# Two blocks for the two parts of a split operand: where the FFNs' inputs and gated products lie in SBUF

## The chip, the cores and the metric

The kernel runs on one core of one Trainium2 chip. The metric is the device time of one execution in microseconds; the median of three runs of the kernel before is 960.75 us (959.98 to 960.87). A change of less than about 0.2% cannot be told from no change.

## What is computed

A trunk of two decoder layers on 256 positions of width 1024, all in float32. Each layer is half an FFN, a mixer and half an FFN again, with a root-mean-square norm ahead of each, and a last norm at the end. The mixer of the first layer is two causal convolutions side by side, that of the second an attention with 16 heads.

```python
def swiglu_ffn(x, w_gate_up, w_down):
    gate, up = jnp.split(x @ w_gate_up, 2, axis=-1)
    return (jax.nn.silu(gate) * up) @ w_down          # 1024 -> 2 x 2816 -> 1024

for layer in range(DEPTH):                            # DEPTH = 2
    x = x + 0.5 * swiglu_ffn(rms_norm(x, ffn1_norm[layer]), ...)
    x = x + mixer(rms_norm(x, mix_norm[layer]), ...)  # layer 0: convolutions, layer 1: attention
    x = x + 0.5 * swiglu_ffn(rms_norm(x, ffn2_norm[layer]), ...)
return rms_norm(x, final_norm)
```

## The kernel before

**Layout.** Everything is kept transposed: 128 channels on the partitions, the 256 positions along the free dimension. A weight tile of 128 x 128 is the stationary operand of a matmul, and 256 positions of activations are the moving one.

**The split.** A float32 operand is split into two float32r parts whose sum is the number: the first part is the number rounded (ScalarE), the second what is left (VectorE). `split` does so for the weights (`w1`, `w2`), `split_to` for activations. Two helpers then multiply split operands. `mm3` (L162, L163, L164) makes three matmuls of 256 columns: w1 by the first part, w1 by the second part, w2 by the first part. `mm2` (L168, L169) makes two: w1 by both parts at once, 512 columns, into the two halves of a PSUM bank, and w2 by the first part, 256 columns. The halves are added later (`join`, or two additions to x).

**Stages.** An FFN is two stages. In the input stage 22 panels multiply `norm.xs`, the split normed input (`xs`, 8 chunks of 128 channels), with gate and up: 16 pairs of mm2 a panel, or 16 triples of mm3 in the panels that `one` picks (L373). The result is scaled, gated and split into `gs`, the gated products (22 chunks). In the product stage each of eight output chunks sums 22 pairs over `gs`, the last one 22 triples. The four FFNs have numbers 0 to 3 in the order in which they run. The attention's queries and keys are also made by mm2 from `xs`, the convolution's inputs mostly by mm3.

**Places.** This is what the change touches. `xs` lies in `xs_all` (L173), a tile that begins at a multiple of 1024 bytes in each partition and is a little longer than needed, so that a stage may begin some bytes later. In `Norm.__init__` (L281) the layout is chunk by chunk: the first part of chunk 0 (256 elements, 1024 bytes), its second part, the first part of chunk 1, and so on. `XS_START` gives the place where this begins, for each FFN's first half (F1), the mixer (MX) and the second (F2), for the two layers. Since a part is 1024 bytes long, each first part and each second part of a stage begins at the same place modulo 1024. `GS_START` does the same for `gs` (L368), whose tile begins at 256 or 320 modulo 1024, so that all parts begin at 1056, that is 32. The weights' tiles begin at multiples of 1024, and so each 128 x 128 weight tile at 0 or 512.

In short, before: parts begin at 288 (inputs of FFNs 0 and 1), 32 (inputs of FFNs 2 and 3, and all products), 192 (the convolution's input), 256 (the attention's input), modulo 1024.

**Order.** `advance` loads units of 1 MB of weights ahead and splits them; SyncE's queue issues the loads. TensorE runs the matmuls in the order in which the code issues them.

Of the kernel before, what the change touches and what calls it, by code (L numbers as in the profile page):

```python
# [11 lines left out]
F32R = mybir.dt.float32r  # L12
# [5 lines left out]
P = 128  # L18
D = 1024
S = 256  # L20
DEPTH = 2
FF = 2816
ND = D // P
NF = FF // P
# [27 lines left out]
ONES = [4, 0, 0, 2]  # L52
ONE_END = 1
PRIO_F = 0
FFN_STEP = 40
# [4 lines left out]
WIDEC = 0  # L60
LINE = 1024
BASE = 16512
XS_START = {"F1": (288, 32), "MX": (192, 256), "F2": (288, 32)}
GS_START = (800, 800, 800, 736)
GROUPS = ((0, 2), (2, 4), (4, 6), (6, 8))
M_POOL = [0, 0, 0, 0]
B_POOL = [0, 0]
# [10 lines left out]
C_F1, C_MX, C_F2, C_FN = 0, DEPTH * ND, 2 * DEPTH * ND, 3 * DEPTH * ND  # L78
# [15 lines left out]
def trunk(ctx: ExitStack, tc: tile.TileContext, xin, wst, cst, bia, idn, out):  # L94
    nc = tc.nc
    keep = ctx.enter_context(tc.tile_pool(name="keep", bufs=1))
# [12 lines left out]
    at = {"load": 0, "split": 0}  # L109
# [20 lines left out]
    def advance(u, ahead_split=ahead_split):  # L130
        while at["load"] < min(n_units, u + ahead_load):
            load(at["load"])
            at["load"] += 1
        while at["split"] < min(n_units, u + ahead_split):
            split(at["split"])
            at["split"] += 1
# [3 lines left out]
    whole = {0} | {first_conv + i for i in WHOLE}  # L140

    class Stream:
        def __init__(self, u):
            self.u = u
# [8 lines left out]
    def take(n):  # L153
        st = Stream(used[0])
        used[0] += n
        return st

    def mm3(o, a, b, start, stop, check=False):
        if len(a) == 1:
            nc.tensor.matmul(o, a[0], b[-1], start=start, stop=stop, skip_group_check=check)  # L160
            return
        nc.tensor.matmul(o, a[0], b[0], start=start, stop=False, skip_group_check=check)  # L162
        nc.tensor.matmul(o, a[0], b[1], start=False, stop=False, skip_group_check=check)  # L163
        nc.tensor.matmul(o, a[1], b[0], start=False, stop=stop, skip_group_check=check)  # L164
# [5 lines left out]


    x = keep.tile([P, ND, S], F32, name="x")
    xs_all = keep.tile([P, ND * 2 * S + LINE // 4], F32R, name="xs")  # L173
    const_all = keep.tile([P, LINE // 4], F32, name="const")
    const = const_all[:, :NCONST]
    ident = keep.tile([P, P], F32, name="ident")
# [101 lines left out]
    class Norm:  # L278


        def __init__(self, col, whole=None, start=0):  # L281
            self.col, self.whole = col, whole
            self.xs = xs_all[:, start // 4:start // 4 + ND * 2 * S].rearrange(
                "p (d t s) -> p d t s", d=ND, t=2)
            self.sums = tmp.tile([P, S], F32, name="sums")

        def add(self, d):
# [23 lines left out]
    def twice(r):  # L311
        return r[:, None, :].to_broadcast([P, 2, S])

    def project(st, base, xs, xg=None):

        bank = psa.tile([P, 2, S], F32, name="pa")
        for i in range(2):
            for k in range(ND):
                w = st.tile(base + 2 * k + i)
                b = (xs[:, k, 0], xs[:, k, 1]) if len(w) == 2 else (xg[:, k],)  # L320
                mm3(bank[:, i], w, b, k == 0, k == ND - 1)
        return bank

    def project2(st, base, xs):

        banks = []
        for i in range(2):
            bank = psa.tile([P, 2, S], F32, name="pa")
            for k in range(ND):
                mm2(bank, st.tile(base + 2 * k + i), xs[:, k], k == 0, k == ND - 1)  # L330
            banks.append(bank)
        return banks
# [31 lines left out]
    def ffn(norm, after, between=None, first=None):  # L364
        _, r = norm.end(True, first is None)
        with tc.tile_pool(name="gp", bufs=1, reuse_waits="tile") as gp:
            st = take(NF)
            start = GS_START[st.u // FFN_STEP] // 4  # L368
            gs = gp.tile([P, NF * 2 * S + start], F32R, name="gs")[:, start:].rearrange(
                "p (f t s) -> p f t s", f=NF, t=2)  # L370
            for p in range(NF):
                advance(st.u + p)
                one = p < ONES[st.u // FFN_STEP] or p >= NF - ONE_END  # L373
                if one:
                    bank = first if first and p == 0 else project(st, p * UT, norm.xs)
                else:
                    banks = project2(st, p * UT, norm.xs)
                with tc.high_priority(offset=PRIO_F):
                    v = tmp.tile([P, 2, S], F32, name="v")
                    if one:  # L380
                        nc.vector.tensor_mul(v, bank, twice(r))
                    else:
                        join(v, banks, r)
                    sl = tmp.tile([P, S], F32, name="sl")
                    nc.scalar.activation(sl, v[:, 0], AF.Silu)  # L385
                    g = tmp.tile([P, S], F32, name="g")
                    nc.vector.tensor_mul(g, sl, v[:, 1])
                    split_to(gs[:, p, 0], gs[:, p, 1], g)
            if between:
                between(gs[:, NF - 1, 0, :1].bitcast(F32))  # L390
            st = take(NF * ND // UT)
            for d in range(ND):
                acc = psb.tile([P, 2, S], F32, name="pb")
                two = d < ND - 1
                for f in range(NF):
                    t = d * NF + f
                    if t % UT == 0 or f == 0:
                        advance(st.u + t // UT)
                    if two:
                        mm2(acc, st.tile(t), gs[:, f], f == 0, f == NF - 1)  # L400
                    else:
                        mm3(acc[:, 0], st.tile(t), (gs[:, f, 0], gs[:, f, 1]), f == 0, f == NF - 1)
                for i in range(2 if two else 1):
                    nc.vector.scalar_tensor_tensor(x[:, d], acc[:, i], 0.5, x[:, d],  # L404
                                                   op0=ALU.mult, op1=ALU.add)
                after.add(d)
# [300 lines left out]
    cold = psb.tile([P, P], F32, name="pb")  # L707
    for _ in range(WARM):
        nc.tensor.matmul(cold, ones, ones, start=True, stop=True)
    norm = Norm(C_F1, start=XS_START["F1"][0])  # L710
    for layer in range(DEPTH):
        nxt = Norm(C_MX + layer * ND, start=XS_START["MX"][layer])
        if layer == 0:
            ffn_first(norm, nxt)
        else:
            ffn(norm, nxt)
        norm, nxt = nxt, Norm(C_F2 + layer * ND, start=XS_START["F2"][layer])
        (conv if layer % 2 == 0 else attention)(norm, nxt)
        if layer < DEPTH - 1:
            norm, nxt = nxt, Norm(C_F1 + (layer + 1) * ND, start=XS_START["F1"][layer + 1])  # L720
            ffn(norm, nxt)
            norm = nxt
    with tc.tile_pool(name="fp", bufs=1, reuse_waits="tile") as fp:
# [7 lines left out]
        for i, (lo, hi) in enumerate(GROUPS):  # L731
            n = hi - lo
# [93 lines left out]
```

## Time and profile before

| | |
|---|---|
| median of three runs | 960.75 us |
| profiled execution, its own time | 960.66 us |
| its span (first to last instruction) | 958.9 us |
| TensorE busy (matmuls) | 945.5 us, 99% |
| VectorE / ScalarE busy | 724.3 us / 543.3 us |
| granted clock of TensorE, mean | 0.997 |
| from HBM | 174 MB, 183 GB/s over the span |

The span is what the trace covers; 1.8 us lie around it. A busy TensorE is not yet one at its peak, since matmuls overlap: the duration of one is longer than the distance from its start to the next one's start. What a matmul costs in a full stream is this distance, which is read from the starts in a timeline or from a count of starts in a stretch.

### The profile page before, as it was taken

How to read it: one execution, taken by the hardware profiler on the slowest of the kernel's cores; microseconds unless marked ns; L12 is line 12 of the kernel's file. 1: busy time of each engine (PE TensorE's matmuls, PEld its weight loads, DVE VectorE, ACT ScalarE, POOL GpSimd, SP SyncE). 2: the span in 40 equal slices, each digit the busy share in tenths (PEclk: the TensorE clock that was granted, in tenths of full speed). 3: DMA queues.
4: the chain of work that ended last, by engine and by line, in shares of the span. 5: the costliest groups of instructions: out<-in, count | busy, mean ns of one | idle time of the engine just before them, and what ended most of it. 6: DMA issues, size and time to landing. Idle time of an engine off the chain costs nothing.

```text
span 958.9 us, 15090 instructions
## 1 busy us (share of the span) xinstructions
PE 945.5 (99%) x5828; PEld 845.8 (88%) x5828; DVE 724.3 (76%) x1373; ACT 543.3 (57%) x975; POOL 47.1 (5%) x61
## 2 busy tenths in 40 slices
PE   8999999999999999999999999999999999999996
PEld 7988898999888888988988889898888998889886
DVE  7988866688879878766788877665698798788552
ACT  6666554488265565554466565444676565665541
POOL 0000000049600000000000000000000000000000
PEclk9999999999999999999999999999999999999998
DMA  8855555544176555555455555555553455555501
GB/s 328 291 205 192 178 206 189 178 159 148 45 260 213 193 207 181 180 211 181 176 194 202 176 191 205 178 195 212 195 191 129 149 186 194 194 202 177 194 26 44
DMA packets 27287, 176.24 MB, mean 184 GB/s; under 512 B 3024, under 2 KB 3792, under 8 KB 6864
## 3 DMA queue, kind: packets, MB, share of 16 engines
q1 hardware_dynamic: 26784, 174.67, 51.7%
q8 instruction: 45, 0.74, 0.3%
q10 hardware_dynamic: 432, 0.63, 0.2%
q14 instruction: 26, 0.21, 0.1%
HBM read 174.23 MB, written 1.05 MB: 183 GB/s over the span
## 4 chain that ended last, share of the span: by engine, by line
PE 90%; POOL 3%; DVE 3%; ACT 1%; DMA 1%; issue 1%; SPq 0%; DVEq 0%; POOLq 0%; ACTq 0%
PE pa L168 33%; PE pa L169 17%; PE pb L168 15%; PE pb L169 8%; PE pa L162 4%; PE pa L163 3%; PE pa L164 3%; POOL yp L486 3%; PE pa L160 2%; PE pb L162 1%; PE pb L163 1%; PE pb L164 1%; DVE pb L463 1%; PE pa L352 1%; PE pb L652 1%
## 5 line engine op out<-in xcount | busy, mean ns | idle before, releaser
L127 DVE TENSOR_TENSOR w<-raw,w 128x1024 fp32r<-128x1024 f32 (+1 forms) x316 | 377.0, 1205 | 136.3 <-ACT w L126 135.9
L168 PE MATMUL pa<-xs,w 128*128 128x512 f32 x1376 | 479.4, 391 | 0.1
L126 ACT CAST w<-raw 128x1024 fp32r<-128x1024 f32 (+1 forms) x316 | 320.5, 1032 | 133.5 <-PE pa L168 49.7
L169 PE MATMUL pa<-xs,w 128*128 128x256 f32 x1376 | 387.2, 282 | 0.0
L168 PEld LDWEIGHTS pa<-xs,w 128*128 128x128 f32 x1376 | 258.1, 188 | 54.9 <-DVE xs L190 0.7
L169 PEld LDWEIGHTS pa<-xs,w 128*128 128x128 f32 x1376 | 260.0, 189 | 0.3
L168 PE MATMUL pb<-gs,w 128*128 128x512 f32 x616 | 213.7, 390 | 0.0
L169 PE MATMUL pb<-gs,w 128*128 128x256 f32 x616 | 173.7, 282 | 0.0
L168 PEld LDWEIGHTS pb<-gs,w 128*128 128x128 f32 x616 | 115.6, 188 | 24.1
L169 PEld LDWEIGHTS pb<-gs,w 128*128 128x128 f32 x616 | 116.4, 189 | 0.0
L385 ACT ACTIVATE sl<-v 128x256 f32<-128x256 f32 x88 | 36.8, 418 | 108.7 <-DVE v L340 104.3
L338 ACT COPY sq<-pa 128x256 f32<-128x256 f32 x172 | 62.9, 366 | 28.6 <-PE pa L169 26.1
L163 PE MATMUL pa<-xs,w 128*128 128x256 f32 x272 | 76.3, 281 | 0.1
L162 PE MATMUL pa<-xs,w 128*128 128x256 f32 x272 | 76.3, 282 | 0.0
L164 PE MATMUL pa<-xs,w 128*128 128x256 f32 x272 | 76.2, 281 | 0.0
L339 DVE TENSOR_TENSOR v<-pa,sq 128x256 f32<-128x256 f32 x156 | 65.5, 420 | 0.0
L404 DVE SCALAR_TENSOR_TENSOR x<-pb,x 128x256 f32<-128x256 f32 x60 | 25.4, 423 | 42.5 <-PE pb L169 28.5
L189 ACT ACTIVATE xs<-x,const 128x256 fp32r<-128x256 f32 x48 | 24.3, 506 | 55.2 <-DVE x L404 43.1
L486 POOL TENSOR_TENSOR yp<-yp,prod 128x256 f32<-128x256 f32 x55 | 45.1, 822 | 208.8 <-ACT prod L485 204.8
L340 DVE TENSOR_TENSOR v<-v,rr 128x512 f32<-128x512 f32 x78 | 53.6, 688 | 0.0
L162 PEld LDWEIGHTS pa<-xs,w 128*128 128x128 f32 x272 | 51.4, 190 | 0.3
L163 PEld LDWEIGHTS pa<-xs,w 128*128 128x128 f32 x272 | 51.1, 188 | 0.5 <-DVE xs L190 0.3
(155 smaller groups left out, 900.7 us busy)
## 6 DMA issues: line engine op xcount, KB each, us to landing
raw<-wst SPq DMA_DIRECT2D x159, 1024.0 KB, 4.8
bt<-bia SPq DMA_DIRECT2D x8, 384.0 KB, 3.3
raw<-wst SPq DMA_DIRECT2D x7, 256.0 KB, 6.3
raw<-wst SPq DMA_DIRECT2D x2, 512.0 KB, 5.6
x<-xin SPq DMA_DIRECT2D x3, 256.0 KB, 5.7
out<-y SPq DMA_DIRECT2D x2, 256.0 KB, 2.5
out<-y ACTq DMA_DIRECT2D x2, 256.0 KB, 2.4
x<-xin SPq DMA_DIRECT2D x2, 128.0 KB, 3.2
```

The source lines that it names most:

```text
L126: nc.scalar.copy(w1[u][:, c], raw[u][:, c])
L127: nc.vector.tensor_sub(w2[u][:, c], raw[u][:, c], w1[u][:, c].bitcast(F32))
L162: nc.tensor.matmul(o, a[0], b[0], start=start, stop=False, skip_group_check=check)
L163: nc.tensor.matmul(o, a[0], b[1], start=False, stop=False, skip_group_check=check)
L164: nc.tensor.matmul(o, a[1], b[0], start=False, stop=stop, skip_group_check=check)
L168: nc.tensor.matmul(o, w[0], b, start=start, stop=False, skip_group_check=True)
L169: nc.tensor.matmul(o[:, 0], w[1], b[:, 0], start=False, stop=stop, skip_group_check=True)
L338: nc.scalar.copy(h, bank[:, 1])
L339: nc.vector.tensor_add(v[:, i], bank[:, 0], h)
L340: nc.vector.tensor_mul(v, v, twice(r))
L385: nc.scalar.activation(sl, v[:, 0], AF.Silu)
L486: nc.gpsimd.tensor_add(yp[:, c], yp[:, c], t)
```

## The change

The two parts of a stage's operand no longer alternate chunk by chunk. All first parts of a stage form one block and all second parts another. A new helper `blocks` makes the view, with a place modulo 1024 for each block. The first block begins where the parts began before. The second begins elsewhere, in each FFN stage at another distance from the first:

| stage | pairs of mm2 | first part at | second part at | distance |
|---|---|---|---|---|
| FFN 0, input / products | 272 / 154 | 288 / 32 | 352 / 96 | 64 / 64 |
| FFN 1, input / products | 336 / 154 | 288 / 32 | 416 / 160 | 128 / 128 |
| FFN 2, input / products | 336 / 154 | 32 / 32 | 48 / 64 | 16 / 32 |
| FFN 3, input / products | 304 / 154 | 32 / 32 | 288 / 544 | 256 / 512 |
| convolution's input | - | 192 | 192 | 0 |
| attention's input | 128 | 256 | 256 | 0 |

The moving operand of L168, one run of 512 elements before, is now two runs of 256 elements. The instructions of all engines stand in the same order as before, with the same waits; only places and access patterns differ. `xs_all` and `gs` grow by 2 KB or a little more, and the tiles behind `xs_all` move by 2048 bytes, which leaves their places modulo 1024. `THREE` is empty, so the lines with it do what they did.

```diff
-XS_START = {"F1": (288, 32), "MX": (192, 256), "F2": (288, 32)}
-GS_START = (800, 800, 800, 736)
+XS_AT = {'F1': ((288, 352), (32, 48)), 'MX': ((192, 192), (256, 256)), 'F2': ((288, 416), (32, 288))}
+GS_AT = ((32, 96), (32, 160), (32, 64), (32, 544))
+GS_BASE = (256, 256, 256, 320)
+THREE = ()
...
+    def blocks(t, base, at, n):
+
+
+        lo = (at[0] - base) % LINE
+        step = n * S * 4 + (at[1] - at[0]) % LINE
+        a = t[:, lo // 4:(lo + 2 * step) // 4].rearrange("p (t q) -> p t q", t=2)
+        return a[:, :, :n * S].rearrange("p t (k s) -> p k t s", k=n)
...
-        def __init__(self, col, whole=None, start=0):
+        def __init__(self, col, whole=None, at=(0, 0)):
             self.col, self.whole = col, whole
-            self.xs = xs_all[:, start // 4:start // 4 + ND * 2 * S].rearrange(
-                "p (d t s) -> p d t s", d=ND, t=2)
+            self.xs = blocks(xs_all, 0, at, ND)
...
-            start = GS_START[st.u // FFN_STEP] // 4
-            gs = gp.tile([P, NF * 2 * S + start], F32R, name="gs")[:, start:].rearrange(
-                "p (f t s) -> p f t s", f=NF, t=2)
+            n = st.u // FFN_STEP
+            gs = blocks(gp.tile([P, NF * 2 * S + 3 * LINE // 4], F32R, name="gs"), GS_BASE[n],
+                        GS_AT[n], NF)
```

## Rows read from the trace of the kernel before

**Rows 1.** The page: engines with busy time; TensorE's granted clock in 40 slices.

```profile
PE 945.5 (99%) x5828; PEld 845.8 (88%) x5828; DVE 724.3 (76%) x1373; ACT 543.3 (57%) x975; POOL 47.1 (5%) x61
...
PEclk9999999999999999999999999999999999999998
```

**Rows 2.** The page: the chain that ended last, by engine and by line.

```profile
PE 90%; POOL 3%; DVE 3%; ACT 1%; DMA 1%; issue 1%; SPq 0%; DVEq 0%; POOLq 0%; ACTq 0%
PE pa L168 33%; PE pa L169 17%; PE pb L168 15%; PE pb L169 8%; PE pa L162 4%; PE pa L163 3%; PE pa L164 3%; POOL yp L486 3%; PE pa L160 2%; PE pb L162 1%; PE pb L163 1%; PE pb L164 1%; DVE pb L463 1%; PE pa L352 1%; PE pb L652 1%
```

**Rows 3.** Waits of the matmuls: total us, times, longest us.

```profile
PE pa L352 <- DVE xg L348: 1.9, 1, 1.9
PE pb L240 <- DVE wide L239: 1.6, 1, 1.6
```

**Rows 4.** The page's groups: count | busy us, mean ns | idle before.

```profile
L168 PE MATMUL pa<-xs,w 128*128 128x512 f32 x1376 | 479.4, 391 | 0.1
...
L168 PE MATMUL pb<-gs,w 128*128 128x512 f32 x616 | 213.7, 390 | 0.0
```

**Rows 5.** Timeline, FFN 0's input stage, matmuls: start us, duration us.

```profile
40.11 0.39 PE L168 MATMUL pa<-xs,w 128*128 128x512 f32 x1
40.34 0.28 PE L169 MATMUL pa<-xs,w 128*128 128x256 f32 x1
40.45 0.39 PE L168 MATMUL pa<-xs,w 128*128 128x512 f32 x1
...
42.19 0.39 PE L168 MATMUL pa<-xs,w 128*128 128x512 f32 x1
```

**Rows 6.** L168 alone in 52.0 us of each FFN stage: matmuls, then weight loads.

```profile
34.00:86.00 52.00, 52.00 (x151) 28.16 (x150) 1.00 0.64 223
132.00:184.00 52.00, 52.00 (x151) 28.16 (x151) 1.00 0.55 199
...
889.00:941.00 52.00, 52.00 (x151) 28.09 (x150) 1.00 0.25 92
```

**Rows 7.** Timeline, the attention's values (weights move): ten matmuls of 512 columns.

```profile
664.69 0.39 PE L162 MATMUL pa<-w,xs 128*128 128x512 f32 x1
...
666.96 0.39 PE L163 MATMUL pa<-w,xs 128*128 128x512 f32 x1
```

**Rows 8.** Timeline, FFN 0's products, last output chunk (mm3): fifteen matmuls.

```profile
184.95 0.28 PE L164 MATMUL pb<-gs,w 128*128 128x256 f32 x1
185.07 0.28 PE L162 MATMUL pb<-gs,w 128*128 128x256 f32 x1
185.19 0.28 PE L163 MATMUL pb<-gs,w 128*128 128x256 f32 x1
...
186.70 0.28 PE L164 MATMUL pb<-gs,w 128*128 128x256 f32 x1
```

**Rows 9.** Timeline, the attention's output (mm3, moving operand at 256): twelve matmuls.

```profile
755.10 0.28 PE L164 MATMUL pa<-o,w 128*128 128x256 f32 x1
...
756.54 0.28 PE L164 MATMUL pa<-o,w 128*128 128x256 f32 x1
```

**Rows 10.** Timeline, queries and keys (mm2, moving operand at 256), an early step.

```profile
678.07 0.40 PE L168 MATMUL pa<-xs,w 128*128 128x512 f32 x1
678.30 0.28 PE L169 MATMUL pa<-xs,w 128*128 128x256 f32 x1
678.41 0.40 PE L168 MATMUL pa<-xs,w 128*128 128x512 f32 x1
...
679.00 0.28 PE L169 MATMUL pa<-xs,w 128*128 128x256 f32 x1
679.12 0.40 PE L168 MATMUL pa<-xs,w 128*128 128x512 f32 x1
```

**Rows 11.** The same in a later step, same places: first and last start of five pairs.

```profile
705.45 0.39 PE L168 MATMUL pa<-xs,w 128*128 128x512 f32 x1
...
707.19 0.39 PE L168 MATMUL pa<-xs,w 128*128 128x512 f32 x1
```

**Rows 12.** Timeline, FFN 0's input stage, weight loads beside rows 5.

```profile
40.11 0.19 PEld L169 LDWEIGHTS pa<-xs,w 128*128 128x128 f32 x1
40.34 0.19 PEld L168 LDWEIGHTS pa<-xs,w 128*128 128x128 f32 x1
```

**Rows 13.** VectorE's second parts, ns min/median/max, and who waited for xs: us, times.

```profile
L190 DVE SCALAR_TENSOR_TENSOR xs<-x,const,xs x48: 478/484/493, 4.4 to 770.0; 128x256 fp32r<-128x256 f32 x48
...
  PEld pa L168: 0.7, 2
  PEld pa L163: 0.3, 1
...
L187 DVE TENSOR_TENSOR gs<-g,gs x88: 414/418/433, 30.3 to 891.8; 128x256 fp32r<-128x256 f32 x88
```

**Rows 14.** All engines in 52.0 us of FFN 1's input stage: PE, PEld, DVE, ACT, POOL.

```profile
300.00:352.00 52.00, 52.00 (x302) 46.10 (x301) 44.57 (x73) 32.02 (x59) 0.00 (x0) 1.00 0.60 206
```

More of the change, by code (lines that the diff above doesn't have):

```diff
@@ L172, in trunk @@
     x = keep.tile([P, ND, S], F32, name="x")
-    xs_all = keep.tile([P, ND * 2 * S + LINE // 4], F32R, name="xs")
+    xs_all = keep.tile([P, ND * 2 * S + 3 * LINE // 4], F32R, name="xs")
     const_all = keep.tile([P, LINE // 4], F32, name="const")
@@ L367, in ffn @@
             st = take(NF)
-            start = GS_START[st.u // FFN_STEP] // 4
-            gs = gp.tile([P, NF * 2 * S + start], F32R, name="gs")[:, start:].rearrange(
-                "p (f t s) -> p f t s", f=NF, t=2)
+            n = st.u // FFN_STEP
+            gs = blocks(gp.tile([P, NF * 2 * S + 3 * LINE // 4], F32R, name="gs"), GS_BASE[n],
+                        GS_AT[n], NF)
             for p in range(NF):
                 advance(st.u + p)
-                one = p < ONES[st.u // FFN_STEP] or p >= NF - ONE_END
+                one = n in THREE or p < ONES[n] or p >= NF - ONE_END
                 if one:
@@ L393, in ffn @@
                 acc = psb.tile([P, 2, S], F32, name="pb")
-                two = d < ND - 1
+                two = d < ND - 1 and n not in THREE
                 for f in range(NF):
@@ L709, in trunk @@
         nc.tensor.matmul(cold, ones, ones, start=True, stop=True)
-    norm = Norm(C_F1, start=XS_START["F1"][0])
+    norm = Norm(C_F1, at=XS_AT["F1"][0])
     for layer in range(DEPTH):
-        nxt = Norm(C_MX + layer * ND, start=XS_START["MX"][layer])
+        nxt = Norm(C_MX + layer * ND, at=XS_AT["MX"][layer])
         if layer == 0:
@@ L716, in trunk @@
             ffn(norm, nxt)
-        norm, nxt = nxt, Norm(C_F2 + layer * ND, start=XS_START["F2"][layer])
+        norm, nxt = nxt, Norm(C_F2 + layer * ND, at=XS_AT["F2"][layer])
         (conv if layer % 2 == 0 else attention)(norm, nxt)
         if layer < DEPTH - 1:
-            norm, nxt = nxt, Norm(C_F1 + (layer + 1) * ND, start=XS_START["F1"][layer + 1])
+            norm, nxt = nxt, Norm(C_F1 + (layer + 1) * ND, at=XS_AT["F1"][layer + 1])
             ffn(norm, nxt)
```

## The prediction, made before the changed kernel was run

> **What bounds the kernel now.** I read the page first. TensorE is busy for 945.5 of 958.9 us, and its granted clock stands at full speed in every slice but the last [rows 1]. The chain that ended last lies on TensorE for 90%, and almost all of that is two lines, L168 and L169, the pair of matmuls of mm2 [rows 2]. The waits of the matmuls are a few single ones of 1.9 us and less [rows 3]. So the time is the number of matmuls times the distance from one to the next, and nothing else counts unless it makes TensorE wait. The groups give the numbers: 1376 + 616 = 1992 pairs, of which 128 belong to the attention's queries and keys (8 steps of 16) and 1864 to the four FFNs [rows 4].
>
> The "mean ns" of a group is not the distance, since matmuls overlap (390 and 282 ns for a pair). I take the distance from starts. In the input stage of the first FFN six pairs take 42.19 - 40.11 = 2.08 us, so 346.7 ns each: some 228.3 ns behind the 512-column matmul and 118.3 behind the 256-column one [rows 5]. Eight stretches of 52.0 us, one in each of the FFN stages, hold 151 starts of L168 each, and 52.0/150 is 346.7 ns again: all eight stages run at one pace, with TensorE busy throughout [rows 6]. The 1864 pairs are therefore 646.2 us, two thirds of the time, and **one nanosecond per pair is 1.86 us**, or 0.19%. That is about what a measurement of this kernel can tell from no change (0.2%), so the question is whether a pair moves by a nanosecond.
>
> **What the change does to this.** Engine by engine the instructions stand in the same order as before, with the same semaphore waits. No work is added and none taken away; the DMAs and the queues are the same. What differs is where TensorE's moving operand comes from.
>
> (1) All 1992 matmuls of 512 columns read two runs of 1 KB that lie some KB apart, where they read one run of 2 KB. No row of before shows a moving operand in two pieces, so I bound it. The second 256 columns of an L168 now cost 228.3 - 118.3 = 110.0 ns, and the first 256, taken to cost what a matmul of 256 costs, 118.3. If the second run had to start as a fresh matmul does, it would cost 8.3 ns more: 1992 x 8.3 = **+16.6 us** at most. Below, the values' matmuls in the attention, 512 columns read straight from the weights, come every 22.7/100 = 0.227 us (2.27 us for ten), 1.6 ns less than L168 [rows 7]: 1992 x 1.6 = -3.2 us. I take **nothing**, for this reason: matmuls of 256 columns under mm3 jump from the first to the second part and back with every instruction (L162, L163, L164) and come every 0.1167 us (1.75 us for fifteen) with a new weight load each [rows 8]; the jump is part of a price that is not above that of L169, which jumps less.
>
> (2) The second part begins at another place modulo 1024 bytes than the first. The first part's place stays (288 or 32 in the inputs, 32 in the products), and so do the weights' (0 or 512). What can come of it? The place of a moving operand does matter here. The attention's output reads 256 columns from places 256 modulo 1024, under the same mm3, and its matmuls come every 0.120 us (1.44 us for twelve) [rows 9] against 0.1167 in the products [rows 8]. Its queries and keys read L168 from 256 as well, and there three pairs take 679.12 - 678.07 = 1.05 to 1.06 us, 353 ns each, in some steps, and 347 (five in 1.74 us) in others [rows 10, 11]. So the place, or how two streams happen to fall, is worth up to 6.7 ns a pair.
>
> The Trainium skill, "TensorE: Matmul & The Clock Gate", section "Step-by-step: what each phase is for", says that TensorE has two independent read ports and that loading the next weights "doesn't steal SBUF read bandwidth from the running matmul". By that rule no place could matter, and the sum would be 0 in every stage; 0.120 against 0.1167 us in the rows differs from it, so the rule is not enough to drop the cases below.
>
> Why I still take nothing: the load of the next weights starts within 0.01 us of a matmul's start (40.11 and 40.11, 40.34 and 40.34) [rows 5, 12], and as mm3 needs one for each 116.7 ns, its stream takes no longer than that. It lies beside the first 256 columns of an L168, whose place does not change, and of an L169, which reads the first part alone. The second 256 columns, the only ones that move, have no load beside them. That is where the 110.0 against 118.3 ns fit.
>
> (3) L163 of mm3 reads the second part with a load beside it: 232 of them in the FFNs (64, 16, 16 and 48 in the inputs, 4 x 22 in the products). Between nothing and 120.0 - 116.7 = 3.3 ns each that is 0 to +0.8 us; as three stages keep a distance of 128 or more, I take 0.3 us. The convolution's L163 keeps its place.
>
> (4) The writes. VectorE writes the second parts, 48 times 484 ns for the inputs and 88 times 418 ns for the products [rows 13]. They read and write 256 contiguous elements as before. Their cover is TensorE's own work: VectorE is busy for 44.57 of 52.0 us in the input stage of the second FFN [rows 14], and TensorE waited for L190 for 1.0 us in all [rows 13]. Were that cover gone, 10% on all 136 writes would be 6 us of VectorE's idle time, of which only the few at the ends of stages could be seen, under 1 us. I take nothing.
>
> The sum is 0 + 0 + 0.3 + 0. The profiled execution took 960.66 us, its span of 958.9 and 1.8 around it, which is 0.1 from the median of 960.75. So **961.0 us**, and for this case alone 959 to 963.
>
> **The rivals.**
> *The jump has a price* (slower). In each L168 the second run begins late, by something between a step that the rows show (1.6 ns, 227 against 228.3) and 8.3 ns. For: nothing in the trace shows a broken stream running at full pace. Against: the jumps between instructions in mm3. I take 3.3 ns, the difference between the paces in rows 8 and 9: 1992 x 3.3 = +6.6, **967 us**. It is slower than before from 1 ns. This would show in all stages alike, the queries and keys included.
>
> *Some stages fall to the other pace* (slower). The same code from the same places ran at 353 and at 346.7 ns in the attention, so the pace is one of a few that a stage settles into, and another place of the second part may settle it into the slower one. For: in rows 10 the distance behind L169 stays at 0.11 to 0.12 us, so that the excess stands behind L168, whose second half is what moves here. Against: all eight stages kept one pace with starts of 288 and of 32 alike. All stages: 1864 x 6.7 = +12.4, 973 us; the two with the small distances, 16 and 32 bytes (336 + 154 pairs), +3.3, **964 us**. It decides from 290 pairs.
>
> *A better fit* (faster). The pace of 346.7 is itself 228.3 + 118.3, while the rows show 226.7 for 512 columns and 116.7 for 256: 343.3 ns together [rows 7, 8]. If a shifted second part brought a pair there, it would give 1864 x 3.3 = -6.2, 954.5 us, and in half of the stages -3.1, **957.6 us**. For: both halves of that pace exist in this kernel. Against: they were never seen in one pair.
>
> *The place means nothing at all* gives the forecast's time and is counted with it.
>
> **How the numbers follow.** Forecast 0.46; price of the jump 0.19; slower pace 0.15; better fit 0.20. Faster by over 0.2% is the third rival, 0.20; slower the first two, 0.34; the rest 0.46. For 8 times in 10 the range must reach into both sides: down to 956 leaves out a better fit in most stages (under 0.1), up to 970 leaves out a jump at its full price and the slow pace in nearly all stages (0.1). So 956 to 970.
>
> **What would show it.** Right: 151 starts of L168's successor in each 52.0 us stretch, and two columns of starts 228 and 118 ns apart as before. The jump's price: the same fewer starts (149 at 3.3 ns) in all eight stretches, 110 ns grown and 118 not. The other pace: 148 in some stretches, 151 in others. A better fit: 152 or 153. If the 118 ns behind L169, whose operand and load stay where they were, changes, then my picture of the load beside the first half is wrong. The prediction fails if the stages change by several ns a pair all in one direction.

## The result, and the profile after

The changed kernel takes **966.1 us** (median of 7, 964.16 to 970.27) against 960.87 us for the kernel before beside it (7, 959.98 to 963.94): 1.0053 times as long, with an interval of 1.0033 to 1.0074. That is 5 us slower. It lies in the range of 956 to 970, but on the other side of the bound of 0.2% than the forecast of 961.0. The profiled execution took 967.74 us with a span of 965.8, which is 6.9 us longer than the span of before.

The page of the kernel after: busy time of each engine, the granted clock by slices, and the first group of mm2. L168 and L169 of before are now L178 and L179 (mm3's three lines: L172 to L174).

```profile
PE 952.5 (99%) x5828; PEld 846.9 (88%) x5828; DVE 724.1 (75%) x1373; ACT 543.3 (56%) x975; POOL 47.2 (5%) x61
PEclk9999999999999999999999999999999999999998
L178 PE MATMUL pa<-xs,w 128*128 128x512 f32 x1376 | 483.3, 394 | 0.0
```

The same 5828 matmuls are busy for 7.0 us longer; VectorE and ScalarE are where they were, and so is the clock [rows 1, 4]. So nearly all of the time is neither a wait nor the clock: the matmuls themselves run at another pace. The waits of the matmuls agree with that: the three longest stand at the places of before [rows 3], with 4.7 us in all against 5.0 (total us, times, longest):

```profile
PE pb L250 <- DVE wide L249: 1.6, 1, 1.6
PE pa L170 <- DVE ya L542: 1.6, 1, 1.6
PE pa L361 <- DVE xs L200: 1.5, 1, 1.5
```

L361 is the line that waited for 1.9 us as L352; L170's wait, 1.5 us before, is shown in the last section.

Where the pace changed is read as in [rows 6]: starts of L178 in 52.0 us of each stage, from the trace of the kernel after. The columns are the stretch, its length, PE's busy time with the count of starts, PEld's, the granted clock, the DMA share and GB/s. The order is the input and product stages of FFN 0, 1, 2, 3.

```profile
53.00:105.00 52.00, 52.00 (x151) 28.11 (x151) 1.00 0.54 189
132.00:184.00 52.00, 52.00 (x151) 28.11 (x150) 1.00 0.56 200
317.00:369.00 52.00, 52.00 (x149) 27.75 (x148) 1.00 0.52 182
411.00:463.00 52.00, 52.00 (x149) 27.74 (x148) 1.00 0.55 191
505.00:557.00 52.00, 52.00 (x148) 27.66 (x148) 1.00 0.53 185
598.00:650.00 52.00, 52.00 (x149) 27.65 (x148) 1.00 0.53 190
807.00:859.00 52.00, 52.00 (x151) 28.16 (x151) 1.00 0.53 191
894.00:946.00 52.00, 51.90 (x150) 28.16 (x151) 1.00 0.27 99
```

The four stages of FFN 1 and FFN 2 hold 148 or 149 starts, the others 150 or 151 as before. A count is coarse by one, so the pace itself comes from a timeline of the same trace (start, duration, engine, line): five pairs in the input stage of FFN 1, then sixteen in that of FFN 2.

```profile
340.08 0.40 PE L178 MATMUL pa<-xs,w 128*128 128x512 f32 x1
...
341.84 0.40 PE L178 MATMUL pa<-xs,w 128*128 128x512 f32 x1
```
```profile
529.85 0.40 PE L178 MATMUL pa<-xs,w 128*128 128x512 f32 x1
...
535.50 0.40 PE L178 MATMUL pa<-xs,w 128*128 128x512 f32 x1
```

1.76/5 = 352.0 ns a pair in FFN 1 (its products too), and 5.65/16 = 353.1 in FFN 2 (353.3 over most of both its stages), against 346.7 [rows 5]. Averaged over a stage, a pair of FFN 2's input is 235.7 ns behind L178 and 117.5 behind L179, where it was 228.3 and 118.3. In FFN 1's input it is 233.2 and 118.8, in FFN 2's products 234.1 and 119.1. So most of the excess stands behind the matmul whose second half moved, and up to 0.8 ns of it behind the other. The sum: 336 x 5.3 = 1.8, 154 x 5.3 = 0.8, 336 x 6.6 = 2.2 and 154 x 6.6 = 1.0, together **5.8 us**. The stages' own lengths in the two traces grew by 1.62, 0.93, 2.16 and 1.07 us, 5.8 again; FFN 0's two stages grew by 0.21 and 0.07, the convolution's by 0.06, FFN 3's by nothing, the start of the program by 0.31 and its tail by 0.46. In the tail the last matmuls ran at a granted clock of 0.51 instead of 0.74 in the 3 us behind their wait. The triples of mm3 (350.0 ns before) took 352 to 355 in FFN 0 to 2.

### The profile page after: what moved, and what is told of

The parts are those of the page before. It is cut to its first block, busy times and chain, and to the rows that moved or that the text cites. A ratio compares the mean times of both kernels' runs of the same rounds, so it can differ in the third digit from the quotient of the medians.

```text
span 965.8 us, 15090 instructions
## 1 busy us (share of the span) xinstructions
PE 952.5 (99%) x5828; PEld 846.9 (88%) x5828; DVE 724.1 (75%) x1373; ACT 543.3 (56%) x975; POOL 47.2 (5%) x61
## 4 chain that ended last, share of the span: by engine, by line
PE 92%; POOL 3%; DVE 2%; ACT 1%; DMA 0%; issue 0%; SPq 0%; DVEq 0%; POOLq 0%; ACTq 0%
PE pa L178 33%; PE pa L179 17%; PE pb L178 15%; PE pb L179 8%; PE pa L172 4%; PE pa L174 4%; PE pa L173 4%; POOL yp L495 3%; PE pa L170 3%; PE pb L174 1%; PE pb L173 1%; PE pb L172 1%; DVE pb L472 1%; PE pb L661 1%; PE pa L361 1%; DMA x<-xin 0%
## 5 line engine op out<-in xcount | busy, mean ns | idle before, releaser
L178 PE MATMUL pa<-xs,w 128*128 128x512 f32 x1376 | 483.3, 394 | 0.0
L179 PE MATMUL pa<-xs,w 128*128 128x256 f32 x1376 | 386.2, 281 | 0.0
L178 PEld LDWEIGHTS pa<-xs,w 128*128 128x128 f32 x1376 | 258.1, 188 | 59.4 <-DVE xs L200 0.5
L179 PEld LDWEIGHTS pa<-xs,w 128*128 128x128 f32 x1376 | 259.2, 188 | 0.3
L178 PE MATMUL pb<-gs,w 128*128 128x512 f32 x616 | 215.5, 393 | 0.0
L179 PE MATMUL pb<-gs,w 128*128 128x256 f32 x616 | 173.8, 282 | 0.0
L178 PEld LDWEIGHTS pb<-gs,w 128*128 128x128 f32 x616 | 115.6, 188 | 25.4
L179 PEld LDWEIGHTS pb<-gs,w 128*128 128x128 f32 x616 | 116.8, 190 | 0.0
L172 PE MATMUL pa<-xs,w 128*128 128x256 f32 x272 | 76.4, 282 | 0.0
L174 PE MATMUL pa<-xs,w 128*128 128x256 f32 x272 | 76.4, 281 | 0.0
L172 PEld LDWEIGHTS pa<-xs,w 128*128 128x128 f32 x272 | 51.5, 190 | 0.3
```

Source lines behind the costliest of these rows:

```text
L178: nc.tensor.matmul(o, w[0], b, start=start, stop=False, skip_group_check=True)
L179: nc.tensor.matmul(o[:, 0], w[1], b[:, 0], start=False, stop=stop, skip_group_check=True)
```

## Experiments

The first theory after the result: the pace of a stage hangs on where the second parts begin, at few places it is one of several slower paces, and the jump between the blocks is free. The rivals: the jump costs something after all in those stages; or the pace belongs to the stage and not to the place; or the place matters only as a distance between the two parts; or it is a chance of each execution. A place below is always modulo 256 bytes, since distances of 256 and 512 changed nothing in the kernel after, and is written (first part, second part). In all diffs `XS_AT` has F1 for FFN 0 and 2 and F2 for FFN 1 and 3, and `GS_AT` FFN 0 to 3. The diffs show the lines that differ, without what stands between them.

### e1_far: two blocks, all distances multiples of 256

```diff
+XS_AT = {'F1': ((288, 544), (32, 288)), 'MX': ((192, 192), (256, 256)), 'F2': ((288, 800), (32, 800))}
+GS_AT = ((32, 288), (32, 544), (32, 800), (32, 288))
```

> Both blocks stay, but every FFN stage gets a distance that is a multiple of 256 bytes (256, 512 or 768). Theory A (the place of the second part sets the pace, and a multiple of 256 is no change; the jump is free): all eight stages at 346.7 ns a pair, 151 starts of L178 in 52 us, time 960.7 +- 1. Rival B (two blocks cost something by themselves, small distances only more): 0.3 to 0.5% above before, 964 to 966.

960.73 us (10 runs), 0.9998 times the kernel before (0.9988 to 1.0008). FFN 1's input and products in its trace, L178 alone:

```profile
315.00:367.00 52.00, 52.00 (x151) 28.16 (x151) 1.00 0.53 189
407.00:459.00 52.00, 52.00 (x151) 28.16 (x151) 1.00 0.56 200
```

All stages are back at 151 starts and 228.3 + 118.3 ns. The two blocks, the jump of several KB in the middle of 1992 moving operands and the larger tiles cost nothing; the whole 5 us belong to the distances.

### e2_scan: eight other places of the second part

```diff
+XS_AT = {'F1': ((288, 480), (32, 112)), 'MX': ((192, 192), (256, 256)), 'F2': ((288, 512), (32, 40))}
+GS_AT = ((32, 128), (32, 192), (32, 80), (32, 240))
```

> First parts stay at 32 modulo 256, second parts at eight new places modulo 256: 224, 128 (FFN 0), 0, 192 (FFN 1), 112, 80 (FFN 2), 40, 240 (FFN 3), input and product stage each. Theory A (what counts is where the second part lies in 256 bytes): paces between 346.7 and 353.3 ns, those at 8 or 16 bytes off a multiple of 32 (112, 80, 40, 240) at 353; none below 346.7 is known, a pace of 343.3 is what the rows of before would allow. Rival (only the distance in steps of 64 counts): 192 and 64 alike at 346.7, all others 352 to 353. Time 961 to 967.

With the first part at 32, the second at 112 gave 353.3 ns (FFN 2's input), at 224 347.8 (FFN 0's input), and at 0, 40, 80, 128, 192 and 240 346.7. So a few places are slow and none is faster than before; the expectation of a slow pace at 40, 80 and 240 fell, and no rule in the distance alone suggests itself.

Its time of 975.09 us isn't comparable: the program got waits that neither before nor after has, of 3.4 us at the head of FFN 2's and of FFN 3's product stage and of 1.5 us at the head of FFN 2's input stage, and what followed one of them is told in the last section.

### e4_same_and_swapped: the first part moved too

```diff
+XS_AT = {'F1': ((96, 96), (48, 48)), 'MX': ((192, 192), (256, 256)), 'F2': ((160, 160), (224, 224))}
+GS_AT = ((160, 32), (64, 64), (48, 32), (128, 128))
```

> Tells place from distance. Distance 0 at other places in six stages: 96, 160, 48, 224 in the inputs of FFN 0 to 3, 64 and 128 in the products of FFN 1 and 3; swapped places in the products of FFN 0 (160 first, 32 second) and FFN 2 (48, 32). Theory D (only the distance between the two parts counts): the six at 346.7 ns, the swapped ones at 352 and 353. Theory P (place against the weight tiles at 0 and 512 counts): 96 at 346.7, 160 at 352, 48 and 64 at 353, and the swapped ones fast behind L178 and slower behind L179.

With a distance of 0 in six stages, the pace was 346.7 ns at 160, 350.0 at 96 and 48, 351.1 at 128, 353.3 at 64 and 224. So the distance alone isn't what counts: the places of both parts count. Theory P in the form of the expectation missed as well, at 160 (352 expected), 96 (346.7) and 48 (353). FFN 0's input (96), FFN 1's (160) and FFN 1's products (64):

```profile
54.00:106.00 52.00, 52.00 (x149) 27.78 (x150) 1.00 0.54 190
318.00:370.00 52.00, 52.00 (x151) 28.14 (x150) 1.00 0.54 191
411.00:463.00 52.00, 52.00 (x148) 27.64 (x147) 1.00 0.55 194
```

In one of the two swapped stages the excess followed the part: with (160, 32) a pair is 230.3 behind L178 and 123.0 behind L179, so it went mostly to L179, which reads the first part alone. In the other it didn't: (48, 32) gave 351.7 as 234.1 + 117.6. (976.22 us, again with an added wait of 3.3 us, ahead of FFN 2's products. The three product stages with an added wait, at (32, 80), (32, 240) and (48, 32), are the only ones in all runs whose distance is no multiple of 32 bytes. Why the program waits there was not looked into.)

### e5_weights_moved: everything behind the activations moved by 128 bytes

```diff
-    keep.tile([P, P], F32, name="gap2")
+    keep.tile([P, P + 32], F32, name="gap2")
+XS_AT = {'F1': ((160, 160), (160, 176)), 'MX': ((192, 192), (256, 256)), 'F2': ((32, 32), (160, 288))}
+GS_AT = ((160, 224), (32, 160), (32, 64), (32, 32))
+GS_BASE = (384, 384, 384, 448)
```

> All weight tiles begin 128 bytes later, at 128 and 640 modulo 1024. If the pace hangs on where the moving operand lies against the weights that are loaded beside it (theory P), then settings 128 bytes up do what the old ones did: FFN 0 input (160, 160) as (32, 32) 346.7 ns; products (160, 224) as (32, 96) 346.7; FFN 2 input (160, 176) as (32, 48) 353.3; FFN 3 input (160, 288) as (32, 160) 352; and FFN 1 input and FFN 3 products, left at (32, 32), leave 346.7. If the weights have no part in it (theory D or an absolute place): (32, 32) stays at 346.7, (32, 160) at 352, (32, 64) at 353.3.

Against the weights, (160, 160) is now what (32, 32) was, and so on. It had 346.7 ns with mm3's triples at 350, as (32, 32) had. (32, 32) had 346.7 as 229.4 + 117.4 with triples of 351.9, as (160, 160) had. (32, 160) had 230.2 + 123.1, as (160, 32) had; (160, 224) had 346.7 and (160, 288) 352.0, as (32, 96) and (32, 160) have in the kernel after. (32, 64), 351.1, has no run to compare. Only (160, 176) gave 346.7 where (32, 48) had 353.3. FFN 0's input (160, 160) and FFN 1's products (32, 160):

```profile
53.00:105.00 52.00, 52.00 (x152) 28.14 (x151) 1.00 0.56 194
408.00:460.00 52.00, 52.00 (x149) 27.66 (x148) 1.00 0.56 195
```

So it isn't a place in SBUF but the place against what was moved with the gap: the raw weights, their split parts, the working tiles behind them. 965.19 us.

### e6_exchanged: the change's distances in other stages

```diff
+XS_AT = {'F1': ((288, 416), (32, 96)), 'MX': ((192, 192), (256, 256)), 'F2': ((288, 304), (32, 64))}
+GS_AT = ((32, 160), (32, 64), (32, 96), (32, 160))
```

> The changed kernel's distances, handed to other stages: 128 to FFN 0 (both stages) and to the products of FFN 3, 16 to the inputs of FFN 1, 32 to the products of FFN 1 and the inputs of FFN 3, 64 to FFN 2 (both). Theory A (the distance makes the pace, whatever the stage): 352 ns a pair in both stages of FFN 0 and the products of FFN 3, 353.3 in FFN 1 and the inputs of FFN 3, 346.7 in FFN 2; time 960.8 + 0.27 x 5.3 + 0.154 x 5.3 x 2 + 0.49 x 6.6 + 0.30 x 6.6 = 969. Rival (FFN 1 and 2 are slow for a reason of their own): 352 to 353 in FFN 1 and 2, 346.7 elsewhere, 966.

A distance of 128 gave 352.0 ns in three stages that had 346.7 in the kernel after (FFN 0's two, FFN 3's products); 32 gave 353.3 in two; 64 gave 346.7 in both stages of FFN 2, which had 353.3. So the pace goes with the place and not with the stage. One exception: 16, in FFN 1's input, ran at 346.7, so the time is 967.23 us and not 969. FFN 0's input (128), FFN 1's (16), FFN 2's (64) and FFN 3's (32), L178 alone:

```profile
53.00:105.00 52.00, 52.00 (x149) 27.73 (x148) 1.00 0.55 187
317.00:369.00 52.00, 52.00 (x151) 28.11 (x151) 1.00 0.56 194
504.00:556.00 52.00, 52.00 (x151) 28.11 (x150) 1.00 0.55 187
805.00:857.00 52.00, 52.00 (x148) 27.55 (x148) 1.00 0.54 184
```

This trace also answers another rival, that the writes of weights disturb the stream. In FFN 3's products (128) the last split of weights ends at 936.6 us and the last load before it. Behind that no weights are written, VectorE and ScalarE are nearly idle, and the pace stays: 23 pairs in 8.10 us are 352.2 ns. All engines (PE, PEld, DVE, ACT, POOL, clock, DMA, GB/s), then the pairs:

```profile
937.20:946.00 8.80, 8.80 (x52) 7.66 (x51) 1.27 (x3) 0.82 (x2) 0.00 (x0) 1.00 0.00 0
937.77 0.40 PE L178 MATMUL pb<-gs,w 128*128 128x512 f32 x1
...
945.87 0.40 PE L178 MATMUL pb<-gs,w 128*128 128x512 f32 x1
```

### a2_again: the kernel after once more

No edit.

> The changed kernel once more, for the paces of its stages in another execution. If a place fixes the pace: 346.7, 346.7 (FFN 0), 352.0, 352.0 (FFN 1), 353.3, 353.3 (FFN 2), 346.7, 346.7 (FFN 3) ns a pair again, inputs and products. If a stage settles into one of several paces by chance, as the queries and keys of the attention did: another pace in one or two of FFN 1 and 2, which would also account for the spread of its times from 964 to 970 us.

967.37 us. Seven stages ran at or near the pace of the first trace (FFN 1's input at 353.3 instead of 352.0), but FFN 2's products at 350.0 to 350.3 instead of 353.3:

```profile
619.80 0.39 PE L178 MATMUL pb<-gs,w 128*128 128x512 f32 x1
...
621.20 0.39 PE L178 MATMUL pb<-gs,w 128*128 128x512 f32 x1
```

That is four pairs in 1.40 us. So at some distances the same code with the same addresses has more than one pace (128 in FFN 1's input, 32 in FFN 2's products), and a stage keeps its own. FFN 2's products at 350.0 instead of 353.3 save 154 x 3.3 = 0.5 us, and FFN 1's input at 353.3 instead of 352.0 costs 0.4. Whether such stages make the scatter of the changed kernel's times (964 to 970) was not shown, since only single executions are traced. Part of it goes with the clock instead: the run of 970.27 us has a mean granted clock of 0.994, the other six 0.996 to 0.997, and the kernel before has a run of 964.50 us at 0.992 beside e1_far, among twelve of 960.2 to 961.5 us at 0.996 to 0.998.

### e8_weights_32 and e10_raw_left: the weights moved by 32 bytes, with and without the raw ones

```diff
-    keep.tile([P, P], F32, name="gap2")
+    keep.tile([P, P + 8], F32, name="gap2")
+XS_AT = {'F1': ((64, 64), (80, 80)), 'MX': ((192, 192), (256, 256)), 'F2': ((96, 96), (256, 256))}
+GS_AT = ((32, 32), (128, 128), (64, 96), (160, 160))
+GS_BASE = (288, 288, 288, 352)
```

> All weight tiles begin 32 bytes later (32 and 544 modulo 1024); both parts of a stage at one place (distance 0). Theory P (place against the weights): what lies 32 bytes up does as it did. FFN 0 inputs at 64 (32 above the weights) 346.7 ns a pair, where 64 gave 353.3 with the weights at 0; FFN 0 products at 32 (0 above the weights) unlike the 346.7 of before, 347 to 353; FFN 1 inputs at 96 (64 above) 353.3, where 96 gave 350.0; its products at 128 (96 above) 350.0, where 128 gave 351.1; FFN 2 inputs at 80 (48 above) 350; FFN 3 inputs at 256 (224 above) 353. Rival (the absolute place): 353.3 at 64, 346.7 at 32, 350.0 at 96, 351.1 at 128.

In e10_raw_left the gap stands behind the raw weights instead and moves only the split ones, w1 and w2; the places are the same.

```diff
+    gap3 = ctx.enter_context(tc.tile_pool(name="gap3", bufs=1))
+    gap3.tile([P, 8], F32, name="gap3")
```

> As the kernel with weights 32 bytes later, but only the split weights w1 and w2 move; the loaded weights before the split (raw, written by DMA and read by ScalarE and VectorE) stay at multiples of 1024. Theory P (TensorE's own weight loads): the same paces as there: 346.7 (FFN 0 input, 64), 346.9, 353.3 (FFN 1 input, 96), 350.1, 350.3 (FFN 2 input, 80), 353.3, 353.3 to 353.8 (FFN 3 input, 256), 351.1 ns a pair. Rival (the reads of raw or the DMA writes disturb the stream): the paces of distance 0 with the weights at 0: 353.3 at 64, 350.0 at 96, 351.1 at 128.

Both kernels had the same eight paces: 346.7 ns at 64, 346.9 at 32, 350.1 at 80 and 128, 351.1 at 160, 353.1 to 353.3 at 96 and 256 and for (64, 96). All but that of 32, for which there is no run to compare, are those of the place 32 bytes lower with the weights where they were: 64 had 353.3 in e4_same_and_swapped and has now what 32 had; 96 has now what 64 had. FFN 0's input (64) and FFN 1's (96), first in e8_weights_32, then in e10_raw_left:

```profile
53.00:105.00 52.00, 52.00 (x151) 28.16 (x150) 1.00 0.56 192
317.00:369.00 52.00, 52.00 (x148) 27.62 (x147) 1.00 0.53 182
```
```profile
53.00:105.00 52.00, 52.00 (x151) 28.16 (x150) 1.00 0.56 193
316.00:368.00 52.00, 52.00 (x148) 27.62 (x147) 1.00 0.55 185
```

So the place of the raw weights is out, and with it that of the DMAs' writes. What is left is the place of the moving parts against the tiles that TensorE loads, and against the working tiles behind these, which moved along; e11_w1_moved tells these two apart. (970.38 and 969.86 us.)

### e9_w2_moved and e11_w1_moved: only one of the two weights moved

In e9_w2_moved a gap of 128 bytes ahead of w2 moves w2, and the working tiles behind it, against the activations. In e11_w1_moved w1 is moved by 128 bytes, and w2 behind it by 1024, so that it stays.

```diff
+    gap3 = ctx.enter_context(tc.tile_pool(name="gap3", bufs=1))
+    gap3.tile([P, 32], F32, name="gap3")
+XS_AT = {'F1': ((288, 416), (32, 192)), 'MX': ((192, 192), (256, 256)), 'F2': ((288, 320), (32, 32))}
+GS_AT = ((32, 160), (32, 64), (32, 192), (160, 32))
+GS_BASE = (384, 384, 384, 448)
```

> Only the second weight parts (w2, loaded while L178 streams) begin 128 bytes later; w1 stays at 0 and 512. Theory P2 (L178's two halves collide, if at all, with the load of w2): (32, 160), which ran at 352 ns a pair in FFN 0 of the exchanged kernel, now lies as (160, 32) does against w2, so L178 takes the 230 ns that (160, 32) had and L179, whose first part lies against w1 as ever, its 118: about 348 in both stages of FFN 0. FFN 1 at (32, 64) as (160, 192): not 353.3. FFN 3 products at (160, 32): L178 as in (32, 160), 233 ns. Rival (the halves collide with the load of w1, or only with each other): (32, 160) stays at 352.0 and (32, 64) at 350 to 353.3.

```diff
+    gap3.tile([P, 32], F32, name="gap3")
+    gap4 = ctx.enter_context(tc.tile_pool(name="gap4", bufs=1))
+    gap4.tile([P, 224], F32, name="gap4")
+XS_AT = {'F1': ((288, 416), (32, 32)), 'MX': ((192, 192), (256, 256)), 'F2': ((288, 320), (160, 288))}
+GS_AT = ((32, 160), (32, 64), (32, 192), (160, 160))
```

> Only the first weight parts (w1) begin 128 bytes later; w2 stays at 0 and 512. Theory P1 (the second half of L178 collides with the load of the next w1, so its place against w1 counts): (32, 160), 32 against w1, fast at 346.7 ns a pair in both stages of FFN 0; (32, 64), 192 against w1, fast in both of FFN 1; (32, 32), 160 against w1, slow at 352 to 353 in the inputs of FFN 2; (32, 192), 64 against w1, slow in its products; (160, 32), 160 against w1, slow in the inputs of FFN 3. Theory D (the distance from the first to the second part, with the weights setting only whether the first part fits): (32, 160), (32, 64) and (160, 32) slow, (32, 32) and (32, 192) fast, as they were with w2 moved.

| place | neither moved | w2 by 128 | w1 by 128 |
|---|---|---|---|
| (32, 32) | 346.7 | 346.7 | 350.0 |
| (32, 64) | 353.3, 350.2 | 353.2 | 350.0 |
| (32, 160) | 352.0, 353.3 | 353.3 | 346.7 in the input, 353.3 in the products |
| (32, 192) | 346.7 | 346.7 | 348.9 |

All theories of one load against one half fell. Moving w2 left these four places near what they were, and moving w1 changed each of them in one stage or in both, so w1's place counts, with w2 and the working tiles where they were modulo 1024. But w2's place does something too: mm3's triples changed with it (356 ns at (32, 32) against 350), and (160, 32), 353.3 as 230.3 + 123.0 ns with nothing moved, stayed slow in both kernels but became 235.3 + 118.0 with w2 moved, so that its excess changed sides. That is the one forecast of theory P2 that came near. FFN 0's input and products, both (32, 160), in e11_w1_moved:

```profile
53.00:105.00 52.00, 52.00 (x151) 28.05 (x151) 1.00 0.56 195
133.00:185.00 52.00, 52.00 (x148) 27.59 (x148) 1.00 0.52 189
```

(970.06 and 968.42 us.) **Open:** which load meets which half of a moving operand, why only these paces come out, and what decides between two paces at one place.

### e12_128_alone: one part of the change alone

Only FFN 1's distances of 128 remain; all others are multiples of 256.

```diff
+XS_AT = {'F1': ((288, 544), (32, 288)), 'MX': ((192, 192), (256, 256)), 'F2': ((288, 416), (32, 288))}
+GS_AT = ((32, 288), (32, 160), (32, 288), (32, 544))
```

> One part alone: FFN 1 keeps its distance of 128 bytes, inputs and products; all other stages get a distance that is a multiple of 256. Theory A: 352.0 ns a pair in FFN 1, 346.7 elsewhere, (336 + 154) x 5.3 = +2.6 us, 963.3 to 963.5; at a pace of 353.3 in one execution or another, +3.3. Rival (a slow stage costs less than its pace, since the next stage starts with more weights ready): below +1.5.

964.72 us (6 runs, 963.32 to 966.03), 1.0038 times the kernel before (1.0026 to 1.0051). FFN 1's input, its products and FFN 2's input, L178 alone:

```profile
316.00:368.00 52.00, 52.00 (x148) 27.65 (x148) 1.00 0.51 183
410.00:462.00 52.00, 52.00 (x149) 27.76 (x148) 1.00 0.54 195
504.00:556.00 52.00, 52.00 (x151) 28.16 (x150) 1.00 0.54 190
```

FFN 1's two stages ran at 353.3 and 352.0 ns and grew by 2.14 and 0.95 us, FFN 2 is back at 346.7. The 3.1 us of these stages make up the profiled execution's 963.69, 2.9 us above the 960.78 of the kernel before. Three of the six runs lie at 963.3 to 963.8 and three at 965.6 to 966.0, some 2 us apart. The longer ones have a mean granted clock of 0.994 to 0.996 and the shorter ones 0.997; there is no trace of the longer ones.

### e7_mixers_32: can a place make it faster?

This is the kernel before, with the mixers' inputs at the place that the FFNs have.

```diff
-XS_START = {"F1": (288, 32), "MX": (192, 256), "F2": (288, 32)}
+XS_START = {"F1": (288, 32), "MX": (32, 32), "F2": (288, 32)}
```

> The kernel before with one constant changed: the mixers' inputs at 32 too, instead of 192 (convolution) and 256 (attention). Theory P: the convolution's 128 triples go from 353 to 350 ns and the queries' and keys' 128 pairs from 350.8 to 346.7 on average, 0.4 + 0.5 = 0.9 us less: 959.9, hardly to be told from before. Rival (their paces come from what runs beside them): no change, 960.8.

The paces came as expected, the time didn't: 961.15 us (11 runs), 1.0006 times the kernel before (0.9997 to 1.0015). The queries' and keys' pairs went from 350.8 to 347.3 ns (four in 1.39 us) and the convolution's triples from 353.3 to 350.0. But the values' matmuls, where xs is the stationary operand and the weights move, went from 227 [rows 7] to 233 ns (ten in 2.33 us):

```profile
665.08 0.40 PE L163 MATMUL pa<-w,xs 128*128 128x512 f32 x1
...
667.41 0.40 PE L164 MATMUL pa<-w,xs 128*128 128x512 f32 x1
```

So this place, which suits xs as the moving operand, is worse for it as the stationary one. The convolution gained nothing from its triples either, since the end of that stage hangs on other engines: the chain that ended last lies there on GpSimd's L486 (3% of the span, [rows 2]) and then on VectorE. TensorE's wait for VectorE near the stage's end was over 62.4 us behind the stage's first matmul in the kernel before and 62.5 us here, and it only grew longer, from 1.5 to 1.9 us. In the traced execution the stage even lost 1.7 us in the way that the last section tells. No kernel here beats the kernel before: 346.7 ns is the lowest pace that any place gave to a pair.

## Where the prediction was right and where it was wrong, step by step

The time lies in the stated range of 956 to 970, but not by the mechanism that was forecast: the range reached up to 970 to leave room for two rivals, and what was held for likeliest, 959 to 963, was missed.

**What bounds the kernel**: right. TensorE's pace is the time, and the 5.8 us come from 980 pairs alone; "one nanosecond per pair is 1.86 us" priced it.

**(1) The jump, taken as nothing**: right. In e1_far all 1992 pairs jump and the ratio is 0.9998. The reasoning from mm3's jumps held, and the rival with a price on the jump (967 us) gave nearly the measured time for a wrong reason: it asked for the same loss in all eight stages, and four of them show none. One of the step's figures is off: the ten matmuls of [rows 7] take 227.0 ns each, so the step against 228.3 is 1.3 ns and not 1.6, which moves two bounds and the third rival's 343.3 by 0.3 ns.

**(2) The second part's place, taken as nothing**: this is the step that failed. Its argument was that "the second 256 columns, the only ones that move, have no load beside them". The measured price was 0 in four stages, 5.3 ns a pair in two and 6.6 in two. The trace shows when a weight load starts, within 0.01 us of a matmul [rows 5, 12], but not when it reads, and I took the start for the whole. The row itself shows a load of 0.19 us [rows 12], longer than the 118.3 ns of the first half. I shortened it to 116.7 by mm3's pace, which shows how often loads follow one another and not when one reads. With the start as evidence the second half is alone; but most of the excess stood behind the matmul with this half (233.2 to 235.7 against 228.3 ns, and 117.5 to 119.1 behind L179). And the pace hangs on where the weights lie: 353.3 became 346.7 at 64 with the weights moved by 32 bytes, and (32, 160) became 346.7 in one stage with w1 alone moved. So the matmul with this half isn't free of the weights' place; which load meets which half was not shown. The test that I named, a change in the 118 ns, was too narrow: they moved by 0.8 ns at most, and the picture was wrong all the same.

The rows to doubt it were there. The values in [rows 8 to 10] showed that a place is worth 3.3 ns a matmul or 6.7 a pair, and I set against them that "all eight stages kept one pace with starts of 288 and of 32 alike". But 288 and 32 are one place modulo 256, as e1_far and FFN 3 show, so the eight stages were one sample and not eight.

The Trainium skill, "SBUF — State Buffer", section "Who interferes with whom", gives TensorE two read ports of SBUF, "1 = matmul moving operand, 1 = LDWEIGHTS, independent". The traces do not bear that out for the time of the two reads: at full clock and with no wait a pair with its parts at 64 took 353.3 or 346.7 ns by the place of the weights (in e4_same_and_swapped and e8_weights_32). The prediction had doubted a like rule, and then dropped its doubt for the picture of the two halves.

**(3) mm3's second parts**, taken at 0.3 us: the right sign, and half the size. Triples grew by 2 to 5 ns in FFN 0, 1 and 2, some 0.6 us over the program. The growth doesn't stand behind the matmul that reads the second part alone: in FFN 0's input the distances behind the three went from 116.9, 117.0 and 116.3 ns to 117.3, 117.9 and 118.1. The reason given counts three stages with a distance of 128 or more; there are four.

**(4) VectorE's writes, taken as nothing**: right. L197 and L200 of the kernel after (L187 and L190 before) take 418 and 483 ns, as in [rows 13]; L197's line gives the shortest, the median and the longest:

```profile
L197 DVE TENSOR_TENSOR gs<-g,gs x88: 411/418/422, 30.6 to 898.2; 128x256 fp32r<-128x256 f32 x88
```

**The rivals.** "Some stages fall to the other pace" is what happened, and its price of 6.7 ns was right (5.3 to 6.6). Its 964 us counted only the distances 16 and 32, as the small ones; 128 fell too, 490 pairs x 5.3 = 2.6 us more, and 964 + 2.6 is the measured 966 to 967. That 64 stayed and 128 did not was in no view of before. "A better fit" did not happen for the pairs: no FFN stage of any kernel ran under 346.7 ns. Triples did go lower, in the convolution, as the last section shows. The chance of 0.15 for the right rival was low because step (2) was believed; its own evidence, the excess behind L168 in [rows 10], pointed at the matmul with the half that was about to be moved.

## What to carry to other kernels

Where matmuls with new weights follow one another without a gap, the place of the moving operand against the weight tiles was worth 2% of a pair's time here (346.7 to 353.3 ns), and more of a triple's (340 in e9_w2_moved, 360 in e4_same_and_swapped). So read the pace from starts stage by stage, and leave a good place alone when a layout is changed (here distances of multiples of 256 bytes kept it). An operand in two runs far apart cost TensorE nothing here. A faster matmul pays only in a stage whose end hangs on TensorE. Stages that share one place modulo that step are one sample, however many there are.

## What the runs showed of the hardware that was not expected

**Few paces, and two at one place.** In 13 kernels the pairs of the FFNs ran at 346.7, 348 to 349, 350 to 352 or 353.3 ns and at nothing below; a stage keeps its pace, and at the distances 16, 32 and 128 two executions or two stages had different ones. Triples spread wider. In e9_w2_moved, with the first and second parts of the convolution's input at 192 as ever and w2 moved by 128 bytes, twelve matmuls take 1.36 us, 113.3 ns each, so 340 ns a triple:

```profile
230.16 0.28 PE L176 MATMUL pa<-xs,w 128*128 128x256 f32 x1
...
231.52 0.28 PE L176 MATMUL pa<-xs,w 128*128 128x256 f32 x1
```

The kernel before has 353.3 in the same stretch, and its best triples in the FFNs take 350.0. A short stretch of the convolution (17 triples from 200 us on) ran at 353.3 in the trace of the kernel after and at 340.8 in a2_again, the same kernel. The gain of e9_w2_moved ended in a longer wait, of 3.0 us, at the place where e7_mixers_32 waited; it was over 62.4 us behind the stage's first matmul there too.

**A short wait can be followed by half the clock.** In e2_scan the first matmul of FFN 2's product stage waited 3.40 us for ScalarE's last write of gs. Timeline of its trace (in brackets the wait), and the window behind the wait (all engines: PE, PEld, DVE, ACT, POOL, clock, DMA, GB/s):

```profile
598.14 0.80 PE L178 MATMUL pb<-gs,w 128*128 128x512 f32 x1 [3.40 <-ACT gs L196]
598.95 0.63 PE L178 MATMUL pb<-gs,w 128*128 128x512 f32 x1
```
```profile
597.70:601.10 3.40, 2.96 (x9) 2.58 (x10) 1.42 (x2) 0.39 (x1) 0.00 (x0) 0.50 0.34 94
```

Behind the wait the granted clock is 0.50, 1.2 instead of 2.4 GHz, and a pair takes 0.64 us. In e7_mixers_32 a wait of 1.9 us in the convolution was followed by the same, and so were the 3.0 us in e9_w2_moved, while 1.5 us at this place in the kernel before and 1.2 to 1.8 in the other traces were not. The wait in the kernel before, then the wait and the stretch behind it in e7_mixers_32:

```profile
PE pa L160 <- DVE ya L533: 1.5, 1, 1.5
```
```profile
PE pa L160 <- DVE ya L533: 1.9, 1, 1.9
```
```profile
255.40:258.90 3.50, 3.50 (x11) 2.76 (x10) 2.05 (x5) 0.00 (x0) 0.73 (x1) 0.54 0.41 164
```

Eleven matmuls in 3.5 us at a clock of 0.54; the kernel before has 18 in the same stretch at 1.00. The length of a wait alone doesn't decide it: 1.9 us at the start of the kernel before (L352, [rows 3]) were followed by a clock of 1.00. Still, here 0.4 us of a wait became 1.7 us of stage time, more than the better place gave back to the convolution.
